# Attention with score rows asked for up to two units ahead, and one slot for both rows of a short unit

## The chip, the cores and the metric

The kernel runs on one core of a Trainium2 chip. The metric is device time in microseconds, the median of several executions; less is better.

## The reference

One decoder layer over 1024 tokens of width 1024, all in float32. What matters here is the attention:

```python
def one_block(i):
    start = i * BLOCK_Q
    qb = lax.dynamic_slice_in_dim(q, start, BLOCK_Q, axis=2)
    cq = lax.dynamic_slice_in_dim(cf, start, BLOCK_Q, axis=2)
    qpos = start + jnp.arange(BLOCK_Q)
    s = jnp.einsum('bhqd,bhkd->bhqk', qb, k, preferred_element_type=jnp.float32) * scale
    s = s + cq[..., :, None] - cf[..., None, :]
    s = jnp.where(kpos[None, :] <= qpos[:, None], s, NEG_INF)
    p = jax.nn.softmax(s, axis=-1)
    return jnp.einsum('bhqk,bhkd->bhqd', p.astype(v.dtype), v)
```

There are 8 heads of width 64, and cf is the running sum of the log of a forget gate. Around it stand a combined projection `h = x @ w_in`, a pooling mixer whose result fills the other half of the width, `x = LN(alpha*x + concat(pool, attn) @ w_out)`, and `x = LN(alpha*x + relu(x @ w_mlp1)^2 @ w_mlp2)`.

## The kernel before, in words

Every float32 factor is split into a high part and a rest (`split`, L70: ScalarE casts at L71, VectorE subtracts at L72), and a product is three matmuls (`three`, L81 to L85). The program has stages: loads and the value projection, three pooling groups, attention, output projection with the first norm, and the two large MLP products, which take from about 345 us to the end.

**Attention's units.** Heads come in four pairs p, each with e = 0, 1. The queries of a head are cut into four units m of 256 queries; unit m sees keys 0 to 256(m+1), so m = 0 and m = 1 are short and m = 3 is long. The list `order` (L635) has 32 units: for pairs 0 to 2 it goes head by head through m = 3, 2, 1, 0 ("falling"); for the last pair it takes both heads of m = 0, then both of m = 1, and so on. Below, unit 2 is the third entry of that list, and so on; units 24 to 31 are the last pair's.

**What a unit does.** `att_probs` (L349) is a generator; each `next` makes one *row*, that is 128 queries: the score matmuls (L369, L370, into PSUM banks `s`, of which there are 3; in the last pair L372 adds the causal mask by one more matmul), a VectorE instruction that adds the gate and keeps the running minimum `nm` (L375), and the ScalarE exponential (L377). The row lies in a slot of the pool "A" (`prob`, L366). There are 9 such slots of 4 KB per partition; the gate rows of a head (L347, a DMA that SyncE issues) and the transposed blocks live there too. `att_values` (L380) then transposes the row blocks on TensorE (L397, banks `pt`, 2 of them), splits them (ScalarE L398, VectorE L399), multiplies by the values (L416, bank `pv`, 1 of them), and writes 256 columns to DRAM (`mix_dram`, L421 to L423). `row_scales` (L429) inverts the row sums, transposes them (L433), copies them on ScalarE (L435) and writes them to `rin_dram` (L436).

**Which row is asked for when.** The loop (L638) runs one unit's `att_values` while the *next* unit's rows are made: the first row after the first transposes (`next(ahead, None)`, L403), the second at half of the key blocks (`run(ahead)`, L409). The scheduler that writes the final order of each engine's queue goes by this program order as priority.

**The filler.** `fillstep` (L629) puts pieces of another generator between: for pairs 0 to 2 the projection of the next pair (`qk_proj`, banks `mm`), for the last pair `last_fill` (L475): the last pooling group in two halves (`late_group`), its small product (`late_linear`, L466 to L471, whose result goes to `mix_dram`), loads of output weights (L516), of the norm's rows (L549) and of the mixture (`mixture`, L521: two loads at L524, the reciprocals at L529, VectorE's product at L530, then a split), and the output projection of the first two token blocks (`out_proj`, matmuls `mm<-B,Q`). The latter needs the mixture, and so the DRAM writes of units 24 and 25 and of the late pooling product.

Of the kernel before, what the change touches and what calls it, by code (L numbers as in the profile page):

```python
# [8 lines left out]
F32 = mybir.dt.float32  # L9
# [6 lines left out]
S = 1024  # L16
# [5 lines left out]
NPAIR = NH // 2  # L22
# [3 lines left out]
CH = 512  # L26
# [10 lines left out]
def trunk(ctx, tc, xT, xn, wuqk, wvf, bf, poolw, pscale, wout, g1, b1, w1, w2, g2, b2, out):  # L37
# [13 lines left out]
    def slot(tag, shape, dt=F32R):  # L51
        uid[0] += 1
        return sb.tile([P] + list(shape), dt, tag=tag, bufs=NBUF[tag], name=f"{tag}{uid[0]}")

    def small(shape, tag, dt=F32, bufs=1, pool=None):
        uid[0] += 1
        return (pool or sb).tile(list(shape), dt, tag=tag, bufs=bufs, name=f"{tag}_{uid[0]}")
# [145 lines left out]
    for t in range(4, NT):  # L203
        for half in range(2):
# [4 lines left out]
            k = ASIDE + 2 * (t - 4) + half  # L209
# [49 lines left out]
    def run(gen):  # L259
        for _ in gen:  # L260
            pass
# [81 lines left out]
    def gate_row(h):  # L343
        if h not in gate_rows:
            gate_rows[h] = slot("A", [S], F32)
            rsum[h] = small([P, NT], "rsum", bufs=3)
            nc.sync.dma_start(gate_rows[h], ncf_dram[h : h + 1, :].to_broadcast([P, S]))  # L347

    def att_probs(p, e, m, prob):  # L349


        KS, Q1, Q2 = (part[e] for part in QK[p])
        h = 2 * p + e
        gate_row(h)
        nb = gate_rows[h]
        falling = p < NPAIR - 1
        for i in (2 * m + 1, 2 * m) if falling else (2 * m, 2 * m + 1):
            nk = (i + 1) * P
            n2 = nk if m % 2 else 256 * (m + 1)
            qs = slice(i * P, (i + 1) * P)  # L360
            if falling:
                nc.gpsimd.tensor_tensor(nb[:, qs], nb[:, qs], maskb, ALU.add)  # L362
            prob[i % 2] = pt = slot("A", [S], F32)
            top = BIG
            for a in range(0, nk, CH):
                b = min(n2, a + CH)  # L366
                diag = not falling and a <= i * P < b
                sp = bank("s")[:, : b - a]
                nc.tensor.matmul(sp, Q1[:, qs], KS[:, a:b], start=True, stop=False)  # L369
                nc.tensor.matmul(sp, Q2[:, qs], KS[:, a:b], start=False, stop=not diag)  # L370
                if diag:
                    nc.tensor.matmul(sp[:, i * P - a : (i + 1) * P - a], identb, maskb, start=False, stop=True)  # L372
                b = min(nk, b)
                nm = small([P, 1], "nm", bufs=8)
                nc.vector.tensor_tensor_reduce(pt[:, a:b], sp[:, : b - a], nb[:, a:b], -1.0, top, ALU.add, ALU.min, nm)  # L375
                top = nm
            nc.scalar.activation(pt[:, :nk], pt[:, :nk], AF.Exp, bias=nm, scale=-1.0, accum_out=rsum[h][:, i : i + 1])  # L377
            yield

    def att_values(p, e, m, prob, ahead):  # L380
        h = 2 * p + e
        rows = slice(e * HD, (e + 1) * HD)
        orow = slice((1 - e) * HD, (2 - e) * HD)
        ov = bank("pv")[:, 0:256]

        def turned(jp):
            tp = bank("pt")
            tt = slot("A", [2, CH])
            if jp < m:
                blocks = [(jj * 256 + ii * P, 2 * jp + jj, ii) for jj in range(2) for ii in range(2)]  # L390
                ev = slice(0, CH)
            else:
                blocks = [(P, 2 * jp + 1, 1), (2 * P, 2 * jp, 0), (3 * P, 2 * jp, 1)]
                ev = slice(P, CH)
                nc.gpsimd.memset(tt[:, :, 0:P].bitcast(F32), 0.0)
            for col, j, ii in blocks:
                nc.tensor.transpose(tp[:, col : col + P], prob[ii][:, j * P : (j + 1) * P], ident)  # L397
            nc.scalar.copy(tt[:, 0, ev], tp[:, ev])  # L398
            nc.vector.tensor_tensor(tt[:, 1, ev], tp[:, ev], tt[:, 0, ev].bitcast(F32), ALU.subtract)  # L399
            return tt  # L400

        nxt = turned(0)
        next(ahead, None)  # L403
        for jp in range(m + 1):
            tt = nxt
            if jp < m:
                nxt = turned(jp + 1)
            if jp == (m + 1) // 2:
                run(ahead)  # L409
            fillstep()  # L410
            mov = ((0, 256), (256, CH)) if jp < m else ((256, CH), (0, 256))
            for s in range(2):
                for jj in range(2):
                    j = 2 * jp + jj
                    a, b = mov[jj]
                    nc.tensor.matmul(  # L416
                        ov, V[j][:, h].rearrange("p s d -> p (s d)"), tt[:, s, a:b],
                        start=(j == 0 and s == 0), stop=(j == 2 * m + 1 and s == 1),
                    )
        mx = slot("U", [256], F32)  # L420
        nc.scalar.copy(mx[rows], ov[orow])  # L421
        nc.vector.tensor_tensor(mx[rows], ov[rows], mx[rows], ALU.add)
        nc.sync.dma_start(mix_dram[m, rows, NG + p, :], mx[rows])  # L423
        if p == NPAIR - 1:
            row_scales(h, 2 * m, 2)
        elif m == 0:
            row_scales(h, 0, NT)
# [206 lines left out]

    order = [(p, e, m) for p in range(NPAIR - 1) for e in range(2) for m in (3, 2, 1, 0)]  # L635
    order += [(NPAIR - 1, e, m) for m in range(4) for e in range(2)]
    pend = None
    for n, unit in enumerate(order):  # L638
        p = n // 8
        if n % 8 == 0:  # L640
            if p + 1 < NPAIR:
                gen, pieces, over = qk_proj(p + 1, "mm"), 4 * KT + 1, 28
            else:
                gen, pieces, over = last_fill(), 2 * KT + 2 + 4 * KT, 27
            fill.update(gen=gen, credit=0.0, rate=pieces / over)
        prob = {}
        ahead = att_probs(*unit, prob)
        if pend is None:
            run(ahead)
        if n + 1 < len(order):  # L650
            gate_row(2 * order[n + 1][0] + order[n + 1][1])
        if pend is None:
            for g in EARLY[1:]:
                pool_linear(g, "A")
        fillstep()
        if pend is not None:
            att_values(*pend, ahead)
        pend = (*unit, prob)
        if n % 8 == 7 and n + 1 < len(order):
            run(gen)  # L660
    att_values(*pend, iter(()))
    run(gen)


# [21 lines left out]
    A = {b: (slot("B", [H, CH]), slot("B", [H, CH])) for b in ("A11", "A12")}  # L686
# [514 lines left out]
    for i in range(1, len(chain) + 1):  # L1201
        cur, prev = chain[i] if i < len(chain) else None, chain[i - 1]
        places(i, 0)
        order = ((cur, "p1"), (prev, "p7"), (cur, "p2"), (prev, "p3"), (cur, "p6"), (prev, "p4"), (cur, "p5"))
        if cur is steps[-1]:
            order = tuple((prev, f) for f in ("p7", "p3", "p4")) + tuple((cur, f) for f in ("p1", "p2", "p5", "p6"))
        if cur is None:
            order = tuple((prev, f) for f in ("p3", "p7", "p4"))
# [50 lines left out]
```

## Time and profile before

| | us |
|---|---|
| median of 3 executions (lowest, highest) | 1040.11 (1039.32, 1040.74) |
| the profiled execution's own time | 1042.56 |
| its span, first to last instruction | 1040.8 |
| attention's first and last score matmul starts (L369) | 110.7 and 326.7 |

The profile gives one execution on one core. PE is TensorE's matmuls, PEld its weight loads, DVE VectorE, ACT ScalarE, POOL GpSimd, SP SyncE, which issues the DMAs. A row such as "PEld pv L416 <- ACT A L398: 7.0, 18" says that weight loads for line 416 stood idle until ScalarE's line 398 had written tile A, 7.0 us in 18 cases. "[0.39 <-DVE nm L375]" at the end of a row of the timeline is the idle time of that engine just before the instruction, and what ended it. A busy PE is not a PE at its peak, since matmuls are pipelined: a matmul of 512 columns shows 0.39 us, and the next one starts 0.23 us after it.

### The profile page before, as it was taken

Reading aid. Unit: us, or ns where it says so; the run is one execution under the profiler, and the core shown is the slowest. Engines: PE = TensorE matmul, PEld = TensorE weight load, DVE = VectorE, ACT = ScalarE, POOL = GpSimd, SP = SyncE. Lnnn points to the kernel's source line nnn. Section 1 sums busy time; section 2 is a strip of 40 time slices with the busy share of each in tenths; the row PEclk is TensorE's granted clock in tenths of the full one; section 3 lists DMA queues with packets and bytes.
Section 4 is the critical chain, followed back from the end, with each engine's and each line's share of the span. In section 5 each row is a group of like instructions: output and inputs, shape, how many; then the busy total and the mean of one; then the engine's idle time right before and its main releaser. Section 6 shows DMA issues by size and latency. Waiting matters only on the chain.

```text
span 1040.8 us, 14125 instructions
## 1 busy us (share of the span) xinstructions
PE 1019.3 (98%) x4976; PEld 847.3 (81%) x4976; DVE 757.1 (73%) x1300; ACT 514.1 (49%) x823; POOL 154.7 (15%) x267
## 2 busy tenths in 40 slices
PE   9999999999999999999999999999999999999996
PEld 9988888888768888887888888888788888888884
DVE  4776678677767887989778778888775666565547
ACT  4623666666664332676766766668521221122152
POOL 0200112111100031112122121120100000000047
PEclk9999999999999999999999999999999999999998
DMA  9702311112585523239667667665989888878753
GB/s 352 279 28 85 113 59 36 40 40 58 176 273 150 183 113 102 75 131 362 241 260 265 224 261 262 223 252 197 350 285 307 285 259 286 275 224 272 238 187 121
DMA packets 113670, 206.29 MB, mean 198 GB/s; under 512 B 9592, under 2 KB 78008, under 8 KB 113600
## 3 DMA queue, kind: packets, MB, share of 16 engines
q1 hardware_dynamic: 94608, 137.63, 41.1%
q0 software_dynamic: 18560, 67.12, 16.6%
q8 instruction: 39, 0.64, 0.3%
q10 hardware_dynamic: 432, 0.66, 0.2%
q14 instruction: 31, 0.25, 0.1%
HBM read 132.42 MB, written 72.94 MB: 197 GB/s over the span
## 4 chain that ended last, share of the span: by engine, by line
PE 50%; issue 4%; DVE 3%; DMA 1%; POOL 1%; SPq 0%; ACT 0%; DVEq 0%; POOLq 0%
PE s L1060 15%; PE pv L1060 8%; PE s L727 8%; PE mm L727 6%; PE pt L727 6%; PE pv L727 4%; PE pt L1060 2%; PE mm L1060 2%; DMA hid_dram<-A 1%; DMA A<-hid_dram 1%; DVE B L72 1%; POOL hid_dram L852 0%; POOL A L720 0%; SPq L1039 0%; DVE A L850 0%
## 5 line engine op out<-in xcount | busy, mean ns | idle before, releaser
L71 ACT CAST B<-S 128x1024 fp32r<-128x1024 f32 (+1 forms) x78 | 67.8, 881 | 163.2 <-PE s L1060 62.8
L727 PE MATMUL s<-B,Q 128*128 128x512 f32 x492 | 116.4, 389 | 0.2 <-ACT B L71 0.2
L727 PEld LDWEIGHTS s<-B,Q 128*128 128x128 f32 x492 | 92.3, 188 | 19.7 <-ACT B L71 0.7
L72 DVE TENSOR_TENSOR B<-S,B 128x1024 fp32r<-128x1024 f32 (+1 forms) x78 | 78.0, 1008 | 31.0 <-ACT B L71 30.8
L1060 PE MATMUL s<-B,Q 128*128 128x512 f32 x390 | 94.7, 389 | 0.0
L1060 PE MATMUL s<-B,A 128*128 128x512 f32 x333 | 84.0, 397 | 2.3 <-DMA A<-hid_dram 2.3
L1060 PEld LDWEIGHTS s<-B,Q 128*128 128x128 f32 x390 | 73.2, 188 | 15.5
L71 ACT CAST Q<-S 128x1024 fp32r<-128x1024 f32 x53 | 55.7, 1051 | 57.3 <-PE s L727 17.0
L852 POOL DMA_DIRECT2D hid_dram<-A x90 | 48.1, 537 | 221.4 <-ACT A L849 164.5
L1060 PEld LDWEIGHTS s<-B,A 128*128 128x128 f32 x333 | 63.1, 190 | 17.1 <-DMA A<-hid_dram 2.7
L72 DVE TENSOR_TENSOR Q<-S,Q 128x1024 fp32r<-128x1024 f32 x53 | 65.6, 1238 | 15.2 <-ACT Q L71 14.7
L727 PE MATMUL pt<-B,Q 128*128 128x512 f32 x312 | 74.6, 389 | 0.0
L727 PE MATMUL mm<-B,Q 128*128 128x512 f32 x300 | 71.6, 389 | 0.0
L727 PEld LDWEIGHTS pt<-B,Q 128*128 128x128 f32 x312 | 58.5, 188 | 12.1
L727 PEld LDWEIGHTS mm<-B,Q 128*128 128x128 f32 x300 | 56.3, 188 | 11.7
L377 ACT ACTIVATE A<-A,nm 128x1024 f32<-128x1024 f32 (+7 forms) x64 | 49.7, 777 | 32.3 <-DVE nm L375 31.0
L416 PE MATMUL pv<-A,B 128*128 128x256 f32 x320 | 62.2, 295 | 2.8 <-DVE A L399 1.2
L416 PEld LDWEIGHTS pv<-A,B 128*128 128x128 f32 x320 | 51.0, 188 | 17.1 <-ACT A L398 7.0
L399 DVE TENSOR_TENSOR A<-pt,A 128x512 fp32r<-128x512 f32 (+1 forms) x80 | 49.6, 634 | 15.1 <-ACT A L398 14.5
L850 DVE TENSOR_TENSOR A<-A,A 128x1024 f32<-128x1024 f32 x45 | 53.6, 1220 | 0.0
L362 POOL TENSOR_TENSOR A<-A,maskb 128x128 f32<-128x128 f32 x48 | 23.4, 491 | 190.8 <-DVE nm L375 135.2
L398 ACT CAST A<-pt 128x512 fp32r<-128x512 f32 (+1 forms) x80 | 41.5, 543 | 19.2 <-PE pt L397 18.3
(427 smaller groups left out, 2342.0 us busy)
## 6 DMA issues: line engine op xcount, KB each, us to landing
hid_dram<-A POOLq DMA_DIRECT2D x105, 512.0 KB, 4.0
S<-in_w_dram SPq DMA_DIRECT2D x62, 512.0 KB
Q<-hid_dram SPq DMA_DIRECT2D x101, 256.0 KB
A<-hid_dram SPq DMA_DIRECT2D x79, 256.0 KB
S<-in_wuqk_dram SPq DMA_DIRECT2D x12, 512.0 KB
wo_dram<-Q POOLq DMA_DIRECT2D x10, 512.0 KB, 3.8
B<-wo_dram SPq DMA_DIRECT2D x10, 512.0 KB
A<-ncf_dram SPq DMA_DIRECT2D x8, 512.0 KB
```

Source lines behind the costliest of these rows:

```text
L71: nc.scalar.copy(hi, src)
L72: nc.vector.tensor_tensor(lo, src, hi.bitcast(F32), ALU.subtract)
L362: nc.gpsimd.tensor_tensor(nb[:, qs], nb[:, qs], maskb, ALU.add)
L377: nc.scalar.activation(pt[:, :nk], pt[:, :nk], AF.Exp, bias=nm, scale=-1.0, accum_out=rsum[h][:, i : i + 1])
L398: nc.scalar.copy(tt[:, 0, ev], tp[:, ev])
L399: nc.vector.tensor_tensor(tt[:, 1, ev], tp[:, ev], tt[:, 0, ev].bitcast(F32), ALU.subtract)
L416: nc.tensor.matmul(ov, V[j][:, h].rearrange("p s d -> p (s d)"), tt[:, s, a:b], start=(j == 0 and s == 0), stop=(j == 2 * m + 1 and s == 1),)
L727: nc.tensor.matmul(dst, b[x][:, k], A[a][y][:, k], start=first and k == 0 and i == 0, stop=k == H - 1 and i == 2, skip_group_check=not first,)
L850: nc.vector.tensor_tensor(x, x, hi.bitcast(F32), ALU.subtract)
L852: nc.gpsimd.dma_start(hid_dram[self.u, :, i, AT[name] : AT[name] + 2 * CH], part.rearrange("p q n t -> p (q n t)"))
L1060: nc.tensor.matmul(dst, h[:, p_], w[q_], start=first and u == self.us[0] and j == 0, stop=u == self.us[-1] and j == 2, skip_group_check=no ...
```

## The change

`att_probs` becomes one stream over all 32 units (`all_rows`), and `rows_until(k)` draws from it until k rows have been asked for. `att_values(n)` asks for the next unit's rows at the same two places as before, and at its last key block for `further(n)` rows more: one for n = 2, 10, 18 (the m = 1 unit of each pair's first head; what is drawn is the first row of the next head's m = 3 unit), two for n = 23 to 26, one for n = 27, else none. Gate rows are asked for two units ahead instead of one. A short unit takes one slot "A" for its two rows instead of two slots.

```diff
+        both = slot("A", [2, CH], F32) if m < 2 else None
...
-            prob[i % 2] = pt = slot("A", [S], F32)
+            prob[i % 2] = pt = slot("A", [S], F32) if both is None else both[:, i % 2]
...
-        next(ahead, None)
+        rows_until(due + 1)
...
             if jp == (m + 1) // 2:
-                run(ahead)
+                rows_until(due + 2)
+            if jp == m:
+                rows_until(due + 2 + further(n))
...
+    def further(n):
+
+        n0 = 8 * (NPAIR - 1)
+        if n < n0 - 1:
+            return int(n % 8 == 2)
+        return 2 if n < n0 + 3 else int(n == n0 + 3)
...
-        if n + 1 < len(order):
-            gate_row(2 * order[n + 1][0] + order[n + 1][1])
+        for ahead in order[n + 1 : n + 3]:
+            gate_row(2 * ahead[0] + ahead[1])
```

Here `due` is 2n + 2. The number of instructions on TensorE stays the same (4994 with the weight loads that stand by themselves). The final queues differ at four places: the change of heads within pairs 0, 1 and 2, and the last pair from unit 23 on. Lines of the changed kernel are higher by 1 from L358 on, by 3 at L397 to L399 and by 5 from L416 on (score matmuls L370 and L371, transposes L400, values L421).

TensorE at the change of heads in pair 1, before: the last score matmuls of the first head's m = 0 unit (`s_2038`), the filler (`mm`), and then the three first score groups of the second head's long unit (`s_2079`, `s_2084`, `s_2092`) one behind the other.

```order
L369 MATMUL s_2038<-Q_1198,Q_1199 128x256
L370 MATMUL s_2038<-Q_1198,Q_1200 128x256
L83 MATMUL mm_1925<-B_437,B_1764 128x512
...
L369 MATMUL s_2079<-Q_1201,Q_1202 128x512
L370 MATMUL s_2079<-Q_1201,Q_1203 128x512
L369 MATMUL s_2084<-Q_1201,Q_1202 128x512
L370 MATMUL s_2084<-Q_1201,Q_1203 128x512
L369 MATMUL s_2092<-Q_1201,Q_1202 128x512
L370 MATMUL s_2092<-Q_1201,Q_1203 128x512
...
L416 MATMUL pv_2068<-A_2070,B_389 128x256
L369 MATMUL s_2097<-Q_1201,Q_1202 128x384
```

The same place now (`s_2032` is the m = 0 unit's, `s_2040` to `s_2091` are the long unit's).

```order
L370 MATMUL s_2032<-Q_1198,Q_1199 128x256
L371 MATMUL s_2032<-Q_1198,Q_1200 128x256
L370 MATMUL s_2040<-Q_1201,Q_1202 128x512
L371 MATMUL s_2040<-Q_1201,Q_1203 128x512
L370 MATMUL s_2045<-Q_1201,Q_1202 128x512
L371 MATMUL s_2045<-Q_1201,Q_1203 128x512
L83 MATMUL mm_1924<-B_437,B_1760 128x512
...
L400 MATMUL pt_2076<-ident_63,A_2008 128x128 x3
L370 MATMUL s_2086<-Q_1201,Q_1202 128x512
L371 MATMUL s_2086<-Q_1201,Q_1203 128x512
L370 MATMUL s_2091<-Q_1201,Q_1202 128x384
```

The long unit's first row (two groups) has moved ahead of the filler and of the m = 0 unit's transposes, so that two groups follow each other where there were four.

TensorE in the last pair, from unit 26's first value product (`pv_3171`) to the late pooling product (`mm_3241`), before: half a row of unit 27 (`s_3207`) stands between.

```order
L416 MATMUL pv_3171<-A_3173,B_389 128x256 x4
L369 MATMUL s_3207<-Q_2367,Q_2368 128x512
L370 MATMUL s_3207<-Q_2367,Q_2369 128x512
...
L85 MATMUL mm_3118<-B_437,B_2977 128x512
L416 MATMUL pv_3171<-A_3189,B_402 128x256 x4
L433 MATMUL pt_3230<-ident_63,ri_3228 2x128
L83 MATMUL mm_3241<-Q_3096,U_2982 128x512
```

The same stretch now (the late product is `mm_3251`).

```order
L421 MATMUL pv_3171<-A_3173,B_389 128x256 x4
L370 MATMUL s_3199<-Q_2356,Q_2357 128x512
L371 MATMUL s_3199<-Q_2356,Q_2358 128x512
L370 MATMUL s_3204<-Q_2356,Q_2357 128x256
...
L370 MATMUL s_3212<-Q_2356,Q_2357 128x512
...
L370 MATMUL s_3217<-Q_2356,Q_2357 128x256
...
L421 MATMUL pv_3171<-A_3181,B_402 128x256 x4
L438 MATMUL pt_3240<-ident_63,ri_3238 2x128
L83 MATMUL mm_3251<-Q_3097,U_2970 128x512
```

Both rows of unit 28 (`s_3199` with `s_3204`, `s_3212` with `s_3217`) now stand ahead of the late pooling product, and unit 27's row has gone further up; before, unit 28's rows stood behind it.

ScalarE at the same time, before: the copy of the late group (`mm_3118`), unit 26's output (`U_3224`) and row sums, the split at L71, then the late product's result (L470).

```order
L377 ACTIVATE A_3206,rsum_2973<-A_3206,nm_3211 128x512
L454 COPY Q_3117<-mm_3118 128x512
L421 COPY U_3224<-pv_3171 64x256
L435 COPY row_3232<-pt_3230 2x128
L71 CAST Q_3238<-Q_3117 128x512
L470 ACTIVATE Q_2986<-mm_3241,hsc_1133 128x512
```

And now.

```order
L378 ACTIVATE A_3198,rsum_2817<-A_3198,nm_3208 128x640
L378 ACTIVATE A_3211,rsum_2817<-A_3211,nm_3221 128x768
L426 COPY U_3234<-pv_3171 64x256
L440 COPY row_3242<-pt_3240 2x128
L459 COPY Q_3118<-mm_3119 128x512
L475 ACTIVATE Q_2974<-mm_3251,hsc_1133 128x512
```

Unit 28's two exponentials have come in front of unit 26's output and of the late product's result; the split has gone behind the latter. On SyncE one of the two last loads of output weights (L516) now stands in front of the write of the late product (L471) instead of behind it; the mixture's loads (L524, L529) follow as before.

More of the change, by code (lines that the diff above doesn't have):

```diff
@@ L378, in att_probs, with att_values @@
             yield
-    def att_values(p, e, m, prob, ahead):
+    def att_values(n):
+        p, e, m = order[n]
+        prob, due = probs[n], 2 * n + 2
         h = 2 * p + e
@@ L636, in trunk, with rows_until @@
     order += [(NPAIR - 1, e, m) for m in range(4) for e in range(2)]
-    pend = None
+    probs = [{} for _ in order]
+    all_rows = (None for n, unit in enumerate(order) for _ in att_probs(*unit, probs[n]))
+    asked = [0]
+    def rows_until(k):
+        while asked[0] < min(k, 2 * len(order)):
+            next(all_rows)
+            asked[0] += 1
+    def further(n):
[3 more added lines that the diff above has]
+        return 2 if n < n0 + 3 else int(n == n0 + 3)
     for n, unit in enumerate(order):
@@ L645, in trunk @@
             fill.update(gen=gen, credit=0.0, rate=pieces / over)
[L646 to L649, printed above, removed]
-        if n + 1 < len(order):
-            gate_row(2 * order[n + 1][0] + order[n + 1][1])
-        if pend is None:
+        if n == 0:
+            rows_until(2)
+        for ahead in order[n + 1 : n + 3]:
+            gate_row(2 * ahead[0] + ahead[1])
+        if n == 0:
             for g in EARLY[1:]:
@@ L655, in trunk @@
         fillstep()
-        if pend is not None:
-            att_values(*pend, ahead)
-        pend = (*unit, prob)
+        if n:
+            att_values(n - 1)
         if n % 8 == 7 and n + 1 < len(order):
             run(gen)
-    att_values(*pend, iter(()))
+    att_values(len(order) - 1)
     run(gen)
```

## Prediction

> **What bounds the kernel now.** I read the page's first part, then busy time by stretch of attention, then what the weight loads wait for in the same stretches, then single rows of the timeline.
>
> ```profile
> PE 1019.3 (98%) x4976; PEld 847.3 (81%) x4976; DVE 757.1 (73%) x1300; ACT 514.1 (49%) x823; POOL 154.7 (15%) x267
> core 0: us, PE busy (x) PEld busy (x) DVE busy (x) ACT busy (x) POOL busy (x), PEclk, DMA share, GB/s
> 224.00:268.00 44.00, 43.42 (x262) 36.64 (x261) 30.94 (x80) 28.81 (x64) 9.32 (x24) 1.00 0.22 65
> 268.00:289.00 21.00, 20.65 (x116) 15.93 (x115) 16.08 (x41) 15.35 (x39) 2.31 (x6) 1.00 0.68 222
> 289.00:304.00 15.00, 12.67 (x78) 9.69 (x77) 10.80 (x32) 9.91 (x21) 1.54 (x4) 1.00 0.91 283
> ```
>
> TensorE sets the time: 98% busy, and a microsecond is to be had only where PE stands idle or its stream has a gap that the modelled ends cover. Attention's 44 us of steady work (224 to 268) hold 36.64 us of weight loads, 83%. The two stretches behind it, where units 22 to 28 run, are thinner: 76% and 65%. At the steady share their loads would need 15.93/0.833 = 19.1 and 9.69/0.833 = 11.6 us, which is 1.9 and 3.4 us less than they take.
>
> The rows of waits of the weight loads name the causes (us in total, times, longest), first for 268 to 289:
>
> ```profile
> PEld pv L416 <- ACT A L398: 0.9, 2, 0.5
> PEld pv L416 <- DVE A L399: 0.7, 1, 0.7
> PEld pt L397 <- ACT A L377: 0.2, 1, 0.2
> ```
>
> For 289 to 304:
>
> ```profile
> PEld pv L416 <- ACT A L398: 1.6, 2, 1.0
> PEld pt L397 <- ACT A L377: 1.5, 2, 0.8
> PEld pt L397 <- DVE A L399: 0.5, 1, 0.5
> PEld s L369 <- DVE nm L375: 0.5, 1, 0.5
> PEld L372 <- issue: 0.4, 2, 0.3
> ```
>
> And the three longest from 304 to 345, around the output projection:
>
> ```profile
> PEld pt L397 <- ACT row L435: 1.0, 1, 1.0
> PEld mm L85 <- DVE Q L72: 0.5, 1, 0.5
> PEld mm L83 <- ACT Q L71: 0.4, 1, 0.4
> ```
>
> So TensorE waits 1.8 us in the first of them and 4.5 us in the second, mostly for its own row's exponential or for the split of its transposes: a short unit leaves it nothing else to do. In the second there is no filler either: between these two rows (start, duration, instruction) no `mm` matmul stands on PE.
>
> ```profile
> 288.05 0.48 PE L83 MATMUL mm<-Q,U 128*128 128x512 f32 x1
> 303.26 0.50 PE L83 MATMUL mm<-B,Q 128*128 128x512 f32 x1
> ```
>
> By PE's own busy time the second stretch lacks only 15 - 12.67 = 2.33 us. [...] But 81% for the whole kernel is no headroom of 19%: a load of 0.19 us stands in a steady pitch of 0.23 (below), so 83% is a full stage here.
>
> **The changes of heads (part a).** The row that moves is work that stands elsewhere on TensorE, so it costs nothing by itself; what goes is the wait for a bank `s` when four groups of scores follow each other with three banks.
>
> ```profile
> 192.98 0.19 PEld L369 LDWEIGHTS s<-Q,Q 128*128 128x128 f32 x1 [0.39 <-DVE nm L375]
> 245.18 0.19 PEld L369 LDWEIGHTS s<-Q,Q 128*128 128x128 f32 x1 [0.40 <-DVE nm L375]
> ```
>
> These are pairs 1 and 2; pair 0 has no such row. With two groups in a row where there were four, both should go: 0.39 + 0.40 = 0.8 us. The bounds are 0 (VectorE, which must now take the same groups within the m = 0 unit, lets TensorE wait there instead) and 1.3 (one more wait for a minimum goes somewhere, as long as the one of 0.5 at L369 above). I take 0.8, since VectorE is busy 30.94 of the 44 steady us and so has room, and the filler, which now follows the moved row, covers what it is late.
>
> **Units 22 to 25 (part b, 268 to 289).** The rows asked for further ahead start only in unit 23. Of the 1.8 us of waits most belong to units whose own row is late by a chain of VectorE, ScalarE and transposes that another row of matmuls would cover. A short unit's row is worth this much PE time (pitches of the score matmuls, from start to start):
>
> ```profile
> 289.50 0.39 PE L370 MATMUL s<-Q,Q 128*128 128x512 f32 x1
> 289.73 0.28 PE L369 MATMUL s<-Q,Q 128*128 128x256 f32 x1
> 289.85 0.28 PE L370 MATMUL s<-Q,Q 128*128 128x256 f32 x1
> 289.97 0.23 PE L372 MATMUL s<-maskb,identb 128*128 128x128 bf16 x1
> 290.04 0.50 PE L397 MATMUL pt<-ident,A 128*128 128x128 f32 x3
> ```
>
> 0.23 for 512 columns, 0.12 for 256, and 0.07 for the mask's: 2 x 0.23 + 2 x 0.12 + 0.07 = 0.77 us for a row of unit 28. But the covering row is taken from later units, which then have less of their own; I take 0.5 of the 1.8, between 0 and 1.8.
>
> **Units 26 to 29 (part c, 289 to 304).** Two rows of unit 28, 2 x 0.77 = 1.5 us, stand ahead of the late product now, so they no longer fill the stretch behind it; what goes is the waiting for exponentials (1.5), since the rows are a unit old when their transposes come, and the bank wait (0.5). The waits on the splits at L398 and L399 (1.6 + 0.5) stay: the transposes and their splits are asked for as before. That is 2.0 of 4.5 (1.5 if the stretch holds only the 3.4 us of the share of loads). TensorE by itself would thus be earlier by 0.8 + 0.5 + 2.0 = 3.3 us.
>
> **What is late next (part d).** The output projection's second block, at 309.83, cannot start before the mixture is there. This is the chain: SyncE's issues (with the size of one load of output weights from the page), VectorE's product, ScalarE's cast, the matmul; then the traffic in two windows.
>
> ```profile
> 290.93 0.38 SPq L471 DMA_DIRECT2D mix_dram<-Q  x1
> 291.40 0.91 SPq L516 DMA_DIRECT2D B<-wo_dram  x2
> 294.19 0.84 SPq L524 DMA_DIRECT2D S<-mix_dram  x2
> ```
>
> ```profile
> B<-wo_dram SPq DMA_DIRECT2D x10, 512.0 KB
> ```
>
> ```profile
> 307.47 1.23 DVE L530 TENSOR_TENSOR S<-S,S 128x1024 f32<-128x1024 f32 x1 [0.67 <-issue]
> 308.73 1.05 ACT L71 CAST Q<-S 128x1024 fp32r<-128x1024 f32 x1 [0.57 <-DVE S L530]
> 309.83 0.50 PE L83 MATMUL mm<-B,Q 128*128 128x512 f32 x1
> ```
>
> ```profile
> 290.00:292.00 2.00, 1.34 (x10) 0.99 (x9) 1.66 (x4) 1.76 (x4) 0.00 (x0) 1.00 0.24 75
> 296.00:302.00 6.00, 5.07 (x34) 3.84 (x32) 4.10 (x14) 3.66 (x8) 0.31 (x1) 1.00 0.97 393
> ```
>
> The DMA engines are nearly empty at 290 to 292 (75 GB/s) and full at 296 to 302 (393 GB/s, 97%). What the mixture reads thus lands a fixed volume after the stream restarts, about 291 in before, and not when TensorE is done. Whatever TensorE saves from 291 to 309 is waited away at 309.83. The restart moves with the late product and its copy:
>
> ```profile
> 289.69 0.62 ACT L71 CAST Q<-Q 128x512 fp32r<-128x512 f32 x1 [0.68 <-POOL Q L461]
> 290.22 0.68 ACT L470 ACTIVATE Q<-mm,hsc 128x512 f32<-128x512 f32 x1
> 292.55 0.83 ACT L377 ACTIVATE A<-A,nm 128x640 f32<-128x640 f32 x1 [0.80 <-DVE nm L375]
> 294.28 0.94 ACT L377 ACTIVATE A<-A,nm 128x768 f32<-128x768 f32 x1
> ```
>
> Earlier by 0.8 + 0.5 (parts a and b), later by 1.5 (unit 28's rows), earlier by 0.68 (the result's copy no longer stands behind the split, which waited that long for GpSimd): 0.5 earlier. The load of output weights that now stands ahead of the late write on SyncE need not wait for that product, and can open the stream as early as parts a and b allow, 1.3 earlier. I take 0.7 between 0.5 and 1.3. Behind SyncE's write nothing new waits but the mixture's loads. Two transposes of a later unit now stand ahead of the block, work of 0.2 to 0.3 (three start at 290.04 and show 0.50 together) that fills the wait; I take 0.2; so this place comes 0.9 earlier, and 3.3 - 0.9 = 2.4 of TensorE's saving is lost in it.
>
> **Behind it (part e).** The wait of 1.0 for the row sums' copy (L435) should go, since unit 27's rows are older, but a wait for the following split or exponential takes most of it (estimate 0.6 from the longest waits of 0.5 to 1.0 above), and of the 0.5 at L85 little changes. I take 0.3, bounds -0.3 and 0.9.
>
> The slot shared by two rows: none of the rows of waits above is one for a slot, and a short unit now needs one fewer, so I cost it at nothing; the work that hides it is the row of the other unit, and without that cover a short unit would wait for both rows' readers, about one wait of 0.5 to 0.8. Gate rows come a unit earlier on SyncE and cost nothing, at 65 GB/s in the steady stretch.
>
> Sum: 0.9 + 0.3 = 1.2 us. The profiled execution's 1042.56 becomes 1041.4; it lies 2.45 above the median of 1040.11, which becomes 1038.9. About 0.2%, or 2.1 us, is what a measurement of this kernel can tell from no change; 1.2 is inside.
>
> **The rivals.** First, faster: the mixture does not bind. That would be so if its reads are issued early enough that the stream opens with parts a and b and the loads ahead of them share the queue. Then the 3.3 stand with e's 0.3: 3.6, giving 1036.5. For it: SyncE's issues at 290.93 to 294.19 follow results of the same units, which come earlier too. Against it: 97% DMA share for six microseconds. Chance 0.25.
>
> Second, slower: ScalarE's queue. Unit 28's two exponentials, 0.83 + 0.94 = 1.8, now stand ahead of unit 26's output and of the late product's copy, and one load of 512 KB ahead of the mixture's takes 0.512/0.393 = 1.3 at the rate of 296 to 302. Both together put the mixture 3.1 later, less the 0.9 that it was to come earlier: 2.2 slower, 1042.3. It decides from the point at which L471's and L524's successors are issued more than 2 us later than 290.93 and 294.19. Against it: the load moved is in the stream either way, ahead of L524 in before too (291.40), so its 1.3 is counted only if the stream does not open earlier. Chance 0.10.
>
> Third, the change doesn't do what it says: the old waits go and as many new ones come, since a row moved ahead is a row missing later; 1040.1. Chance 0.05.
>
> Fourth, the clock. Late in the MLP, PE stands idle for a transfer, and the clock granted behind that is low:
>
> ```profile
> 749.71 2.01 PE L1060 MATMUL s<-B,A 128*128 128x512 f32 x6 [2.30 <-DMA A<-hid_dram]
> 750.00:756.00 6.00, 6.00 (x20) 4.53 (x20) 3.85 (x6) 1.40 (x2) 0.00 (x0) 0.72 0.97 315
> ```
>
> 6 us at 0.72 lose 1.7 us. If an earlier or later arrival there avoids it, the time is 1038.9 - 1.7 = 1037.2; a second dip would cost as much. Chance 0.05, as the change touches nothing there. [...]
>
> **How the numbers follow.** Forecast 1038.9, chance 0.55, own range 1037.9 to 1040.0 (the restart 1.3 instead of 0.7 and e at 0.7: 1037.9; a at 0, which also takes the restart back by 0.8, with e at 0: 1040.0). The rivals to the fast side come to 1036.5 and 1037.2, the slow one to 1042.3. The range reaches down to 1036.5, leaving out the half of the first rival that would gain more than its bare sum (0.12), and up to 1041.0, which leaves out most of the second (0.08). Faster by over 2.1 means below 1038.0: the first rival and the fourth, 0.30. Slower means above 1042.2: the second rival, 0.10. The rest, 0.60, is no change.
>
> **What would show it.** Part a: no bank wait over 0.3 at the two changes of heads. Parts b and c: 268 to 304 with fewer waits for L377's successor, and the waits for the splits still there. Part d: the wait in front of the output projection's second block larger than before, with the DMA stream full up to it and the block 0.9 earlier. The forecast is wrong if that block comes 2 us or more earlier (first rival) or any later (second), or if waits for slots appear. Where the time after that block differs by over 0.5 in either direction, part e or the clock is at fault.

## Result and the profile after

The change makes the kernel slower. The median of the changed kernel is 1047.1 us (1045.73 to 1048.37, 6 runs) against 1039.92 (1039.25 to 1042.15, 6 runs): ratio 1.0064, 95% interval 1.0053 to 1.0075, so 5.5 to 7.8 us. Forecast were 1038.9 and a range up to 1041.0. In what follows one execution of e11 (1401.95 us) and one of the kernel before beside it (1124.05), with mean clocks of 0.675 and 0.849, are left out of the ratios.

The two stretches and the first window of DMA traffic that were shown of before, now after:

```profile
268.00:289.00 21.00, 20.30 (x115) 15.68 (x114) 17.45 (x47) 14.88 (x37) 1.92 (x4) 1.00 0.60 196
289.00:304.00 15.00, 13.60 (x81) 10.02 (x81) 9.16 (x26) 10.15 (x22) 2.06 (x5) 1.00 0.89 308
290.00:292.00 2.00, 2.00 (x14) 1.49 (x13) 0.58 (x2) 1.95 (x6) 0.30 (x2) 1.00 0.65 260
```

PE stands idle 1.40 us in 289 to 304 instead of 2.33: the rows ahead do fill some of it. How much that is worth shows at a place where the same matmuls lie behind TensorE in both kernels, the last transposes ahead of the output projection: 303.04 before, 302.75 after, 0.3 us earlier. The loss is elsewhere. Waits of the weight loads, first 289 to 304, then 304 to 345:

```profile
PEld pv L421 <- ACT A L401: 1.2, 3, 0.7
PEld pt L400 <- ACT row L440: 0.9, 2, 0.7
PEld pt L400 <- DVE A L402: 0.7, 1, 0.7
PEld s L370 <- DVE nm L376: 0.6, 2, 0.3
PEld mm L83 <- ACT Q L71: 0.2, 1, 0.2
```

```profile
PEld pv L421 <- issue: 3.0, 1, 3.0
PEld pv L421 <- DVE A L402: 0.6, 1, 0.6
```

The wait for exponentials (1.5 before) is gone, as forecast, but new waits of 0.9 for the copied row sums (L440) stand in its place: 3.6 in all, and 4.0 with the 0.4 of L373 as before, against 4.5. And there is one wait of 3.0 us that the kernel before doesn't have. Five views at that place show where it is from. SyncE's issues:

```profile
313.31 0.62 SPq L534 DMA_DIRECT2D S<-rin_dram  x1
314.32 0.25 SPq L441 DMA_DIRECT2D rin_dram<-row  x1
316.67 0.38 SPq L476 DMA_DIRECT2D mix_dram<-Q  x1
317.10 0.63 SPq L534 DMA_DIRECT2D S<-rin_dram  x1
```

ScalarE's copy of the second late product, VectorE, and TensorE:

```profile
315.95 0.69 ACT L475 ACTIVATE Q<-mm,hsc 128x512 f32<-128x512 f32 x1 [1.66 <-PE mm L85]
```

```profile
324.54 1.22 DVE L535 TENSOR_TENSOR S<-S,S 128x1024 f32<-128x1024 f32 x1 [3.49 <-DMA S<-rin_dram]
325.98 0.43 DVE L427 TENSOR_TENSOR U<-pv,U 64x256 f32<-64x256 f32 x1
```

```profile
326.56 0.48 PE L421 MATMUL pv<-A,B 128*128 128x256 f32 x2 [2.57 <-DVE U L427]
```

And two windows behind it, with the granted clock in the last column but two:

```profile
328.00:330.00 2.00, 2.00 (x8) 1.72 (x7) 2.00 (x5) 1.02 (x2) 1.45 (x3) 0.50 0.24 72
330.00:332.00 2.00, 2.00 (x12) 1.75 (x11) 1.90 (x4) 1.99 (x3) 0.00 (x0) 0.76 0.95 287
```

And the same place before, SyncE and then VectorE:

```profile
312.55 1.28 SPq L529 DMA_DIRECT2D S<-rin_dram  x2
316.17 0.38 SPq L471 DMA_DIRECT2D mix_dram<-Q  x1
```

```profile
319.87 1.23 DVE L530 TENSOR_TENSOR S<-S,S 128x1024 f32<-128x1024 f32 x1 [0.53 <-DMA S<-rin_dram]
324.36 0.43 DVE L422 TENSOR_TENSOR U<-pv,U 64x256 f32<-64x256 f32 x1
```

The mixture of the second 256 tokens needs two loads of inverse row sums. Before, SyncE issues both from 312.55 on, ahead of the write of the second late pooling product (L471, 316.17). After, the second one stands behind the row write L441 and that late write, which waits until ScalarE has copied the product (315.95, done at 316.64). It is issued at 317.10, where before it was at about 313.2 (312.55 + 1.28/2), and VectorE's product L535 starts 7.4 us later, at 324.54, after a wait of 3.49 us for it. Right behind L535 in VectorE's queue (but for a short step of the norm) stands the add that empties TensorE's only bank `pv` (L427, 325.98). VectorE doesn't take it earlier, though ScalarE has copied the other half of that bank (L426) by 321.2 (320.82 + 0.36). So TensorE waits 2.57 us at 326.56, with its clock at 0.50 and 0.76 in the four microseconds from 328. Matmuls of 512 columns start 0.43 apart there (329.58 to 330.86) and 0.23 apart ahead of the wait (323.15 to 323.60), so an estimate from the two windows is 2 x 0.50 + 2 x 0.24 = 1.5 us more.

This is theory 1. Theory 2 is that the rows further ahead make ScalarE and VectorE late, wherever that load stands.

### The profile page after: what moved, and what is told of

It is laid out like the page before. It is cut to its first block, busy times and chain, and to the rows that moved or that the text cites. A ratio compares the mean times of both kernels' runs of the same rounds, so it can differ in the third digit from the quotient of the medians.

```text
span 1045.2 us, 14121 instructions
## 1 busy us (share of the span) xinstructions
PE 1022.5 (98%) x4976; PEld 848.0 (81%) x4976; DVE 757.6 (72%) x1300; ACT 513.1 (49%) x823; POOL 154.9 (15%) x267
## 4 chain that ended last, share of the span: by engine, by line
PE 50%; issue 4%; DVE 3%; DMA 1%; POOL 1%; SPq 0%; ACT 0%; DVEq 0%; POOLq 0%
PE s L1077 15%; PE pv L1077 8%; PE s L744 8%; PE mm L744 6%; PE pt L744 6%; PE pv L744 4%; PE pt L1077 2%; PE mm L1077 2%; DMA hid_dram<-A 1%; DMA A<-hid_dram 1%; DVE B L72 1%; POOL hid_dram L869 0%; SPq L1056 0%; POOL A L737 0%; DVE A L867 0%
## 5 line engine op out<-in xcount | busy, mean ns | idle before, releaser
L71 ACT CAST B<-S 128x1024 fp32r<-128x1024 f32 (+1 forms) x78 | 67.6, 880 | 164.1 <-PE s L1077 62.0
L71 ACT CAST Q<-S 128x1024 fp32r<-128x1024 f32 x53 | 55.7, 1051 | 57.3 <-PE s L744 17.0
L421 PEld LDWEIGHTS pv<-A,B 128*128 128x128 f32 x320 | 51.4, 189 | 19.5 <-ACT A L401 5.4
L421 PE MATMUL pv<-A,B 128*128 128x256 f32 x320 | 62.0, 295 | 4.8 <-DVE U L427 2.6
L401 ACT CAST A<-pt 128x512 fp32r<-128x512 f32 (+1 forms) x80 | 41.8, 541 | 23.1 <-PE pt L400 22.2
```

The source lines that it names most:

```text
L71: nc.scalar.copy(hi, src)
L421: nc.tensor.matmul(ov, V[j][:, h].rearrange("p s d -> p (s d)"), tt[:, s, a:b], start=(j == 0 and s == 0), stop=(j == 2 * m + 1 and s == 1),)
```

## Experiments

Each row of this table gives the median of the kernel, of the kernel before on the same chip, and the ratio with its interval.

| kernel | us | before | ratio (95%) |
|---|---|---|---|
| e1 both loads of row sums together | 1043.24 | 1040.72 | 1.0020 (1.0009 to 1.0032) |
| e2 rows ahead at changes of heads only | 1040.93 | 1040.72 | 1.0000 (0.9991 to 1.0009) |
| e4 product L535 on GpSimd | 1045.71 | 1040.72 | 1.0049 (1.0035 to 1.0063) |
| e5 before, late load added | 1042.71 | 1040.72 | 1.0017 (1.0008 to 1.0025) |
| e6 e1, half of the norm's rows later | 1043.12 | 1040.45 | 1.0024 (1.0013 to 1.0034) |
| e7 before, norm's rows later | 1041.01 | 1040.45 | 1.0013 (1.0004 to 1.0022) |
| e8 e1 without rows at changes of heads | 1044.11 | 1040.45 | 1.0044 (1.0031 to 1.0058) |
| e10 e1 without unit 28's rows ahead | 1041.80 | 1040.63 | 1.0009 (0.9996 to 1.0022) |
| e11 e1, late product first | 1041.07 | 1040.63 | 1.0003 (0.9992 to 1.0013) |
| e14 the same again | 1041.34 | 1040.47 | 1.0013 (1.0003 to 1.0024) |
| e17 e11 and the norm's rows later | 1041.42 | 1040.47 | 1.0008 (0.9998 to 1.0018) |

### The late load: e1, e5, e4

**e1** keeps every row ahead and puts the two loads together again.

```diff
-                nc.sync.dma_start(rb[e * HD : (e + 1) * HD], rows.to_broadcast([HD, NPAIR, 256]))
+                with tc.high_priority(offset=200 if m == 1 else 0):
+                    nc.sync.dma_start(rb[e * HD : (e + 1) * HD], rows.to_broadcast([HD, NPAIR, 256]))
```

> The changed kernel, but both loads of inverse row sums for the second block's mixture (256 queries m = 1) are issued on SyncE one behind the other, ahead of the second late product's write, as before the change. Theory 1 (the second of the two loads, queued behind that write, lands some 4 us later, VectorE's product waits for it, and the value bank's output add behind it on VectorE holds up TensorE, whose clock then drops): the wait of 2.6 us at about 326 falls under 0.6, the clock stays at 1.00 there, and the time is 1039.5, from 1038 to 1041. Theory 2 (the rows asked for further ahead make ScalarE and VectorE late, wherever that load stands): within 1 of the changed kernel's 1047.1.

Both loads of e1 go out at 313.28, ahead of the late write; then VectorE's product and the add, and the clock:

```profile
313.28 1.28 SPq L535 DMA_DIRECT2D S<-rin_dram  x2
317.08 0.38 SPq L476 DMA_DIRECT2D mix_dram<-Q  x1
```

```profile
321.31 1.22 DVE L536 TENSOR_TENSOR S<-S,S 128x1024 f32<-128x1024 f32 x1
322.64 0.43 DVE L427 TENSOR_TENSOR U<-pv,U 64x256 f32<-64x256 f32 x1
```

```profile
328.00:330.00 2.00, 2.00 (x12) 1.47 (x11) 2.00 (x5) 1.70 (x4) 0.31 (x1) 1.00 0.78 309
```

The wait at 326 is gone and the clock stays at 1.00, as theory 1 has it. But the time, 1043.24, lies between the two theories: about 4 of the 7 us come back, not all. The rest needs a second cause.

**e5** does the harm alone, in the kernel before: the second load waits for the late product's result.

```diff
+    late_mx = []
...
+        if c:
+            late_mx.append(mx)
...
+                if m == 1 and e:
+                    nc.gpsimd.tensor_copy(rb[HD:, 0, 0:1], late_mx[0][HD:, 0:1])
                 nc.sync.dma_start(rb[e * HD : (e + 1) * HD], rows.to_broadcast([HD, NPAIR, 256]))
```

> The kernel before, with one thing added: the second of the two loads of inverse row sums for m = 1 must wait for the second late product's result (a GpSimd copy of one column into its target, read from that result), so that it stands behind that product's write on SyncE, as in the changed kernel. Theory 1: a wait of 1.5 to 3 us for the value bank at about 326 and a lower clock behind it, 1043 to 1047.5. Theory 2: 1040, within 1 of the kernel before.

SyncE, VectorE and TensorE of e5:

```profile
316.31 0.38 SPq L475 DMA_DIRECT2D mix_dram<-Q  x1
317.13 0.63 SPq L535 DMA_DIRECT2D S<-rin_dram  x1
```

```profile
324.19 1.23 DVE L536 TENSOR_TENSOR S<-S,S 128x1024 f32<-128x1024 f32 x1 [2.96 <-DMA S<-rin_dram]
```

```profile
326.10 0.47 PE L416 MATMUL pv<-A,B 128*128 128x256 f32 x2 [1.86 <-DVE U L422]
```

The same chain appears with no row moved, and costs 1.0017 of 1040.72, 1.8 us (0.8 to 2.6). The time is a little under what was expected. In the profile no lower clock follows this shorter wait (1.00 in each window from 322 to 334); in 9 of the 12 timed runs the mean clock is 0.995, which 4 of the 29 of before beside it show, so part of the 1.8 us may be clock.

**e4** takes the product off VectorE, so that the add isn't behind it.

```diff
-            nc.vector.tensor_tensor(mf, mf, rb, ALU.mult)
+            (nc.gpsimd if m == 1 else nc.vector).tensor_tensor(mf, mf, rb, ALU.mult)
```

> The changed kernel, with the second block's product of mixture and inverse row sums moved from VectorE to GpSimd; the late load stays where it is. Theory 1 with its link through VectorE's queue: the load still lands at about 324, but VectorE doesn't wait for it, the wait for the value bank at 326 falls under 0.6, and the time is 1040, from 1038 to 1042. Theory 1 without that link (TensorE needs the mixture itself), or theory 2: 1045 to 1048.

The time of 1045.71 isn't clear of the changed kernel's (the intervals of the ratios overlap), so the expectation of 1040 failed. ScalarE's and TensorE's rows show why:

```profile
327.23 1.04 ACT L71 CAST Q<-S 128x1024 fp32r<-128x1024 f32 x1 [5.01 <-POOL S L535]
328.18 0.58 ACT L401 CAST A<-pt 128x512 fp32r<-128x512 f32 x1
```

```profile
328.81 0.77 PE L421 MATMUL pv<-A,B 128*128 128x256 f32 x2 [2.79 <-ACT A L401]
```

VectorE no longer waits for the load, and now ScalarE does: the cast that follows the product (L71) holds back the next split (L401). The experiment isn't clean, since the product takes 2.36 us on GpSimd (from 324.83) and 1.22 on VectorE, which delays that cast too (325.85 in the changed kernel). But the link isn't VectorE's queue in particular: on both engines a step of the late mixture that stands in front of attention's own work passes the wait on: 3.49 us of VectorE and 2.57 of TensorE in the changed kernel, 5.01 of ScalarE and 2.79 of TensorE here.

### One part alone: e2, e8

**e2** asks for rows further ahead at the changes of heads only; **e8** does so in the last pair only, with the loads together.

```diff
-        n0 = 8 * (NPAIR - 1)
-        if n < n0 - 1:
-            return int(n % 8 == 2)
-        return 2 if n < n0 + 3 else int(n == n0 + 3)
+        return int(n % 8 == 2 and n < 8 * (NPAIR - 1))
```

```diff
-            return int(n % 8 == 2)
+            return 0
```

> The changed kernel with the rows further ahead at the three changes of heads alone (none for the last pair); shared slots and earlier gate rows stay. Theory 1: the two loads stay together ahead of the late write, so no stall at 326; the time is 1039.5, from 1038.5 to 1040.5, with the two waits of 0.4 for score banks gone. Theory 2 (rows ahead in the last pair): the same, 1039.5. Theory 3 (the shared slot of a short unit or the earlier gate rows cost the time): 1044 or more.

> Rows further ahead in the last pair alone (none at the changes of heads), with both loads of row sums together. If the changes of heads are worth what the trace shows (about 0.4 to 0.8 us), this is 0.4 to 0.8 slower than the kernel with the pair together and both sorts of rows ahead: 1043.6 to 1044. If what is still lost comes from the changes of heads: 1040.7. Theories 3 and 4: 1043.2 to 1044.

e2 is the kernel before within 0.1%. So shared slots, earlier gate rows and the changes of heads cost nothing that shows here, and theory 3 as e2's expectation numbers it falls (from e6 on the numbers 3 and 4 stand for other theories). But e2 also misses its range of 1038.5 to 1040.5: no gain by the rows at the changes of heads shows. e8, without them, takes 1044.11, a little over all that was expected, and its interval touches e1's, so it doesn't show a value of these rows either.

The traces say where the gain went. The banks' waits are gone after the change, and TensorE waits for a row's exponential instead (TensorE's weight loads, changed kernel):

```profile
143.84 0.86 PEld L400 LDWEIGHTS pt<-ident,A 128*128 128x128 f32 x8 [0.75 <-ACT A L378]
197.39 0.86 PEld L400 LDWEIGHTS pt<-ident,A 128*128 128x128 f32 x8 [0.31 <-ACT A L378]
249.48 0.86 PEld L400 LDWEIGHTS pt<-ident,A 128*128 128x128 f32 x8 [0.30 <-ACT A L378]
```

A place behind all three changes of heads, with the same matmuls behind it, first before and then after:

```profile
269.11 0.23 PE L372 MATMUL s<-maskb,identb 128*128 128x128 bf16 x1
```

```profile
269.10 0.23 PE L373 MATMUL s<-maskb,identb 128*128 128x128 bf16 x1
```

The score matmul just ahead of the first of these changes starts at 135.89 and 135.88. From there to here it is 133.1 to 133.4 us in the profiles of all kernels here, those with the rows ahead (e2: 133.4) and those without (e8: 133.2).

### What e1 still loses: e6, e7, e9, e10, e11

e1's first output matmul waits for the first mixture: PE row of e1, then the changed kernel's issues of that mixture, which were at 290.93, 294.19 and 295.08 before.

```profile
304.66 0.50 PE L83 MATMUL mm<-B,Q 128*128 128x512 f32 x1 [0.97 <-ACT Q L71]
```

```profile
292.64 0.40 SPq L476 DMA_DIRECT2D mix_dram<-Q  x1
296.91 0.80 SPq L529 DMA_DIRECT2D S<-mix_dram  x2
297.76 1.38 SPq L534 DMA_DIRECT2D S<-rin_dram  x2
```

Theory 3 from here on: unit 28's rows and exponentials, ahead of the late product, start the first mixture's chain late. Theory 4: the loss is in the MLP. **e6** is e1 with this edit, by which one 512 KB load goes behind that mixture's loads, **e7** is the kernel before with it, where both go behind them, **e9** is e1 once more. (In e6, e10, e11, e14 and e17 the loads of row sums are kept together by an offset of 1000 instead of 200.)

```diff
         load_output_weights(4, KT)
-        load_rows()
         mixture(0, 0)
         mixture(0, 1)
+        load_rows()
```

> The kernel with both loads of row sums together (1043.24), and one of the two 512 KB loads of the norm's rows moved on SyncE behind the first mixture's loads; the loads for m = 1 stay together. Theory 3 (what the kernel with the pair still loses, 2.5 us, is the first mixture arriving late: SyncE issues its loads 2.7 us later than before, behind a load of output weights and the late product's write): the wait of 0.97 for the first output matmul at 304.7 falls under 0.3, the time is 1041 to 1042. Theory 4 (the loss is in the MLP, about 750, where TensorE waits for the hidden activations from DRAM, and not in attention): the wait at 304.7 may go, but the time stays at 1043, from 1042.3 to 1044.

> The kernel before, with both loads of the norm's rows (2 x 512 KB) behind the first mixture's loads on SyncE. Theory 3: the product for the output projection's 25th matmul lands earlier, the wait of 0.2 at 309.8 and that of 0.5 at 311.1 go, 0 to 0.7 gain: 1040.2, from 1039.5 to 1041. Theory 4: no change, 1040.7.

> The same kernel as the first experiment (both loads of row sums together), for a second profile of an execution nearer its median of 1043.2, since its profiled execution took 1041.62. Theory 3: against the first profile, the wait at 304.7 before the first output matmul is longer, 1.5 us or more. Theory 4: the attention's end lies within 0.3 us of the first profile's, and the difference is in the wait at about 750 and the clock behind it.

e6 (1043.12) and e7 (1041.01) gained nothing. e9 took 1042.09, with waits of 0.21 and 0.83 for L71 at 303 and 311 against e1's 0.97 at 304.66. e6 and e9 miss theory 3's numbers. e6's time is the one that theory 4 names, but its profile doesn't show a loss in the MLP alone: TensorE waits 1.24 us for the first mixture at 304, with the clock at 0.53 in 304 to 306.

**e10** keeps unit 28's rows where they were, **e11** instead pulls the late product with its copy and write ahead of them.

```diff
-        return 2 if n < n0 + 3 else int(n == n0 + 3)
+        return 2 if n < n0 + 2 else 0
```

```diff
-        late_linear(0, pw)
+        with tc.high_priority(offset=400):
+            late_linear(0, pw)
```

> Both loads of row sums together, and rows further ahead for n = 23 to 25 and at the changes of heads, but none at n = 26 and 27: unit 28's two rows stand behind the late pooling product again. Theory 3 (the 2.5 us that the kernel with the pair together still loses come from the first mixture, whose chain starts late because unit 28's rows, 1.5 us, and their exponentials stand ahead of the late product): the late product's write is issued by 291.5, the waits for L71 in front of the first block fall under 0.4 in sum, the time is 1040 to 1041. Theory 4 (the loss is in the MLP): 1043, from 1042.3 to 1044.

> Both loads of row sums together, all rows further ahead as in the changed kernel, and the first late pooling product with its result's copy and write at a higher priority, so that it stands ahead of unit 28's rows and the write ahead of the last loads of output weights. Theory 3: the first mixture's loads are issued by 295, no wait over 0.4 for L71 in front of the first block, and TensorE keeps what the rows ahead save in 289 to 304: 1038.5 to 1040.5. Theory 4: 1043, from 1042.3 to 1044.

e11 is 1041.07 and level with the kernel before; e10, 1041.80, lies between that and e1. Both miss theory 3's ranges on the slow side and theory 4's on the fast side, and the intervals of e1, e10 and e11 overlap. The medians lean to theory 3, but e10's profile doesn't show its link. The late product's write and the first mixture's loads go out as in the kernel before (291.15 and 294.15, against 290.93 and 294.19), and yet ScalarE's cast waits for that mixture until 304.08, where before it ran at 302.16, and TensorE waits 0.74 us for the cast:

```profile
304.08 1.04 ACT L71 CAST Q<-S 128x1024 fp32r<-128x1024 f32 x1 [1.69 <-DMA S<-mix_dram]
```

One difference is that SyncE issues three loads of output weights just ahead of these loads, where before there were two; whether they are the cause isn't tested.

### Clock and repeats: e12 to e17

> The kernel before once more, for a second profile: its first one, 1042.56, lies 2.5 above its median. If the two states of the wait and clock at about 750 make that difference, an execution near 1040 shows a mean clock of 0.997 and no clock under 0.9 in 748 to 762, with the attention's end as in the first profile within 0.3 us.

> The changed kernel once more, for a second profile. Theory 1: the wait for the value bank at about 326 is there again, between 2 and 3.5 us, with the load of row sums landing at about 324; the attention's end lies within 1 us of the first profile's.

Before again (1040.66) and after again (1046.32). First before: TensorE at a fixed place in the MLP and behind its wait for the hidden activations, then the window 748 to 762.

```profile
477.33 3.02 PE L727 MATMUL pv<-B,Q 128*128 128x512 f32 x12 [1.09 <-DVE A L817]
749.35 1.80 PE L1060 MATMUL s<-B,A 128*128 128x512 f32 x6 [1.46 <-DMA A<-hid_dram]
```

```profile
748.00:762.00 14.00, 12.65 (x54) 10.10 (x55) 11.56 (x18) 6.66 (x10) 0.00 (x0) 1.00 1.02 338
```

Then after, with its wait at 326 ahead:

```profile
326.42 0.53 PE L421 MATMUL pv<-A,B 128*128 128x256 f32 x2 [2.34 <-DVE U L427]
480.37 1.89 PE L744 MATMUL pv<-B,Q 128*128 128x512 f32 x7 [1.08 <-DVE A L834]
752.65 2.47 PE L1077 MATMUL s<-B,A 128*128 128x512 f32 x6 [1.79 <-DMA A<-hid_dram]
```

```profile
748.00:762.00 14.00, 12.21 (x46) 9.27 (x45) 7.25 (x11) 5.40 (x8) 0.00 (x0) 0.88 1.03 340
```

The wait at 326 is there again (2.34). At the MLP's fixed place the changed kernel is 480.37 - 477.33 = 3.0 us late, at the end 1044.5 - 1038.9 = 5.6. Of the 3.0, 0.6 are there already at 135 us, ahead of everything that the change touches (135.74 against 135.17). Executions of one kernel differ by as much (135.89 in before's first), so such places are better counted from there: the fixed place comes after 341.0 and 342.2 us in the two profiles of before, and after 345.1 and 344.6 in those of the changed kernel, 2.5 to 4.1 later.

Of the 2.6 us behind that place, an estimated 14 x 0.12 = 1.7 are a lower clock at 748 to 762, which this execution of before doesn't have, and 0.3 a longer way to the end of the wait for the hidden activations (752.65 - 480.37 against 749.35 - 477.33). The rest, 0.6, isn't resolved. The first profile of before had the lower clock as well (0.72 in 750 to 756, behind a wait of 2.30), which by the same estimate accounts for 6 x 0.28 = 1.7 of the 2.5 us that it lay above its median; so a comparison of the first two profiles (4.4 us) understates the change. All six timed runs of after show mean clocks of 0.991 to 0.996; of the 23 runs of before beside e14, 18 have 0.996 to 0.998 and 5 have 0.995. By the medians that is 0.003 of 1045 us, or 3.1, an estimate from rounded clocks, about as much as the 1.5 at 328 and the 1.7 at 750 together. Whether the change makes the second more likely isn't shown: 6 of the 17 profiles that can be compared have it, two of the kernel before or its variant e7 among them.

**e14** repeats e11, **e15** and **e16** repeat e1, and **e17** is e11 with both 512 KB loads moved as in e7.

> The kernel with both loads of row sums together and the first late pooling product ahead of unit 28's rows, once more, for a profile (the first one fell in an execution at a clock of 0.675) and for a second measurement. Theory 3: the median is again 1040 to 1042, at least 1 us under that of the kernel with the pair alone (1043.2), the first mixture's loads are issued by 295 and TensorE's waits for L71 in front of the first block stay under 0.4 in sum. Theory 4: 1043.

> The kernel with both loads of row sums together, a third profile. Theory 3: the waits for L71 at 304 and 310 add up to 0.5 to 2 us and vary between executions with the landing of the first mixture, and the attention's end lies 0.5 to 1.5 later than in the kernel before (349). Theory 4: the attention's end lies within 0.3 us of 349, and the excess is behind it.

> The same kernel, a fourth profile; theories 3 and 4 as for the third.

> The kernel with both loads of row sums together and the late product first, and both 512 KB loads of the norm's rows behind the first mixture's loads on SyncE: all that the experiments point to, in one kernel. Theory 3: the first mixture lands 1 to 2 us earlier still, TensorE keeps what the rows ahead save (1 to 2 us), and the time is 1038 to 1040. Theory 4: 1041 to 1043.

e15 and e16 took 1041.84 and 1041.23 with waits of 1.11 and of 0.53 and 0.21 for L71 in front of the output projection's first matmuls (303 to 311), and reach the MLP's fixed place at 477.13 and 477.03, level with before's 476.88 and 477.33. Counted from 135 us, the four profiles of e1 (1041.23 to 1042.09) reach it after 341.9 to 342.8 us, before's after 341.0 and 342.2. So the missing 2.5 us don't show in them; the timed runs reach from 1040.90 to 1045.82. e14's profiled execution (1044.88, clock 0.994) shows what the long ones of its own kernel look like, on ScalarE, on TensorE and in two windows:

```profile
305.70 1.04 ACT L71 CAST Q<-S 128x1024 fp32r<-128x1024 f32 x1 [1.89 <-DMA S<-mix_dram]
```

```profile
306.79 0.79 PE L83 MATMUL mm<-B,Q 128*128 128x512 f32 x1 [1.88 <-ACT Q L71]
```

```profile
308.00:310.00 2.00, 2.00 (x8) 1.51 (x7) 0.32 (x2) 1.39 (x3) 0.00 (x0) 0.50 0.92 256
310.00:312.00 2.00, 2.00 (x6) 1.60 (x5) 1.53 (x2) 0.43 (x1) 0.00 (x0) 0.50 0.78 311
```

The first mixture lands late, TensorE waits 1.88 where under 0.4 was expected, and loses an estimated 3 more to the clock (0.54 in 306 to 308 and 0.75 in 312 to 314, around the two windows). In this kernel the late product comes first: its write is issued at 284.03, the mixture's loads at 295.20, and the mixture isn't there before 305.70, 10.5 us later. In e15 and e16, which are e1 again, it was there 6.9 and 6.3 us after its loads (296.57 to 303.47 and 296.69 to 302.99), in e10 9.9 us (294.15 to 304.08). So when it lands isn't set by the late product alone, and theory 3 isn't shown. Nor is a lower clock what most long runs of e1 have: of its 7 runs over 1043 us 5 have a mean clock of 0.996 or 0.997, as most runs of the kernel before have. What e1 still loses stays open.

e17 is the fastest in attention: the MLP's fixed place comes at 475.45, or 340.3 us after the place at 135, 0.7 to 1.8 us before the kernel before. In this one profile the rows ahead are thus worth something once both chains of the mixture are eased. It is given back behind, as TensorE's rows and the window show:

```profile
475.45 3.01 PE L746 MATMUL pv<-B,Q 128*128 128x512 f32 x12 [1.07 <-DVE A L836]
747.77 1.99 PE L1079 MATMUL s<-B,A 128*128 128x512 f32 x6 [1.82 <-DMA A<-hid_dram]
```

```profile
748.00:762.00 14.00, 14.00 (x54) 11.02 (x54) 10.63 (x17) 5.77 (x9) 0.00 (x0) 0.88 0.89 289
```

The wait for the hidden activations (1.82) is in front of the same matmuls as in e12 and e13 (1.46 and 1.79), and the clock in 748 to 762 is 0.88. 7 of its 11 runs have a mean clock of 0.995 or less. The median is 1041.42, in theory 4's range and not in theory 3's, and no better than before. No version here beats the kernel before.

## Why the prediction was wrong

**The step that failed**, and made the kernel slower, is in part d: "Behind SyncE's write nothing new waits but the mixture's loads." That was read at the first late write (L471, 290.93) alone. The change also moves SyncE's queue at the *second* late write (316), where one of two loads went from ahead of a waiting write to behind it. That cost a wait of 2.57 us at 326, with a clock of 0.50 and 0.76 in the windows behind it (1.5 us by the estimate above), a term that the sum doesn't have. The prediction followed that queue only as far as the block at 310. The profile of before already said how tight it was: VectorE's product waited 0.53 us for that load. With the load issued 3.9 us later the product started 4.7 us later in the changed kernel (324.54 against 319.87) and 4.3 in e5 (324.19). With the two loads together again (e1) about 4 of the 7 us come back.

**A second step failed:** TensorE's saving of 0.8 + 0.5 + 2.0 = 3.3 us ahead of the output projection. It came to 303.04 - 302.75 = 0.3.

**Part a** (0.8): no wait for a bank as those at 192.98 and 245.18 shows at the changes of heads after, but waits of 0.75, 0.31 and 0.30 for an exponential stand in their place, and the place at 269 comes no earlier (269.11 and 269.10). That is the third rival, at this place. Pair 0 did have a bank wait, against the prediction's reading, of 0.30 at 139.61. **Part b** (0.5) can't be told from part c. **Part c** (2.0 of 4.5): the exponentials' waits went, 1.5 as forecast, but the row sums' copy (0.9), a bank wait that stayed (0.6 after 0.5) and the mixture's cast (0.2) took most of it: 4.0 is left, 0.5 gained in the row of waits, 0.3 with part b at 303.

**Part d, the first mixture:** the restart was forecast 0.7 earlier and came 292.64 - 290.93 = 1.7 later, its reads 2.7 later (296.91 against 294.19), so the second rival's trigger (more than 2 us) was met by the reads. The loads ahead of the write did open the stream earlier, as forecast (260 GB/s in 290 to 292, after 75), but parts a and b had no 1.3 us to pay for unit 28's rows. The block came at 310.29, 0.46 later and not 0.9 earlier, with a wait of 0.17 in front of it: there was no saving of TensorE's to be lost there. The second rival had the sign, with ScalarE's queue and a load ahead as its mechanism; the main loss was neither, but a load behind a write, at the second mixture.

**The clock**, the fourth rival: it was given 0.05 "as the change touches nothing there". But the clock was lower at another place as well: behind the stall of 2.57 us that the change adds at 326 it was 0.50 and 0.76 in 328 to 332. About 3 of the 7 us are clock by the estimate above; that the other half comes from the change isn't shown. After idle times of 2.57, 1.88 and 1.24 us (after, e14, e6) the windows of two microseconds show 0.50, 0.50 and 0.53 (from 328, 308 and 304), and after 1.86 us in e5 (at 326) and 2.17 in e4 (at 753) they show 1.00. No run here shows what decides between the two.

## What to carry to other kernels

When a change lets a scheduler reorder, read every queue at every place where it differs, DMA issues first: here a load that slipped behind a waiting write was issued 3.9 us later, VectorE's product that waits for it started 4.7 us later, and the add behind that product, which has nothing to do with the load, kept TensorE waiting for 2.57 us. Look for rows in which an engine already waits a few tenths for a load: the 0.53 at 319.87 showed such a place without slack. A wait that goes is no gain until a later place, with the same work behind it, comes earlier: here the banks' waits went and 269.11 stayed. Where a clock steps down after short stalls, compare medians and mean clocks of many runs: here the first profile of before has 0.88 in 748 to 762 and the second 1.00.

## What was not expected of the hardware

The granted clock was 0.53 in 304 to 306 after an idle time of TensorE of 1.24 us (e6) and 0.50 in 330 to 332 after one of 2.79 us (e4, ending at 328.81), but 1.00 in 754 to 760 after 2.17 us (e4, ending at 753.48): in these runs the length of the pause alone doesn't decide. A load of inverse row sums of 256 KB took 7.4 us from issue to the start of VectorE's product (317.10 to 324.54), and 7.1 in e5 (317.13 to 324.19).
